# A log-sum-exp kernel: the wait for the final store moved behind the exit barriers, and the store halved over two queues

## The chip, the cores and the metric

The kernel runs on one core of a Trainium2 chip. The metric is device time in microseconds (us). All runs quoted here are of the fast state, at a granted clock of 1.0. The span in a profile is the time from the first to the last record of one profiled execution. It is about 1.8 us shorter than the time of the same execution (162.2 against 163.96 us for the kernel before), as it leaves out what happens before and after the records.

The engines are named as in the profile: ACT is ScalarE, DVE is VectorE, POOL is GpSimd, SP is SyncE. A name with a q (ACTq, SPq, POOLq) is the instruction queue of that engine, which issues transfers and handles semaphores. A semaphore is a counter that an engine or a transfer raises and that another engine waits on. A packet is one record of a DMA engine at work on a piece of a transfer. A store has landed when the last of its 16 increments has arrived at its semaphore. A drain is the DRAIN instruction that the exit puts ahead of each of an engine's reports.

Times are compared with the kernel before of the same rounds. Each run left one profiled execution, so a duration read from records is that of one execution.

## The reference

```python
# x: 32 x 512 x 1024 float32, axis = -1
x_max = np.max(x, axis=axis, keepdims=True)
return x_max.squeeze(axis) + np.log(np.sum(np.exp(x - x_max), axis=axis))
```

The output is 32 x 512 float32, that is 64 KB. The input is 64 MB. The kernel leaves the maximum out and takes the log of the sum of the exponentials directly.

## The kernel before

Rows are spread as 128 partitions x 128 rows. SyncE loads chunks of rows into a ring. ScalarE takes the exponentials and part of the sums, VectorE the other sums. ScalarE takes the log of the first 67 columns in mid-run and of the last 61 columns at the end, and stores all 128 columns with one transfer. GpSimd waits for it.

```python
    landed = [tc.alloc_semaphore(f"landed{i}") for i in range(len(CHUNKS))]
    act_done = tc.alloc_semaphore("act_done")
    dve_done = tc.alloc_semaphore("dve_done")
    stored = tc.alloc_semaphore("stored")
    # ... (loads, exponentials and sums: the change does not touch them)
    take_logs(logged, NB, dves, acts)          # the last Ln
    nc.scalar.wait_ge(act_done, acts)
    nc.scalar.dma_start(out=out_v, in_=res).then_inc(stored, 16)
    nc.gpsimd.wait_ge(stored, 16)
```

What the text does not show is the exit that the framework appends when its context closes. In the built kernel it reads, for every engine but GpSimd: drain, report to GpSimd, wait for release, and then the same again. GpSimd gathers the reports, releases the others, sets the semaphores that came from `tc.alloc_semaphore` to zero with one range clear, and then gathers and releases a second time. As GpSimd's wait for the store stands ahead of all that GpSimd does there, its part of the exit starts when the store has landed (161.215 us in the trace; the wait is passed at 161.239).

The softmax here doesn't subtract the row's maximum and nothing guards it: scores larger than these inputs give would overflow.

Of the kernel before, what the change touches and what calls it, by code (L numbers as in the profile page):

```python
# [1 line left out]

# [4 lines left out]



CHUNKS = [  # L10
    (4, 1), (15, 11), (16, 10), (16, 15), (16, 0), (14, 0), (12, 9), (9, 5), (7, 5), (5, 4),
    (4, 3), (3, 0), (2, 2), (2, 2), (1, 0), (1, 0), (1, 0),
]
RING_ROWS = 51

LN_AT = 5

FIRST_PARTS = [("sync", 0, 128)]


@with_exitstack
def kernel(
    ctx: ExitStack,
    tc: tile.TileContext,
    x: bass.AP,
    axis: bass.AP,
    out: bass.AP,
):
    nc = tc.nc
    P = nc.NUM_PARTITIONS  # L30

    assert axis in (-1, len(x.shape) - 1), f"only last-axis reduction supported, got {axis}"

    x_flat = x.flatten_outer_dims()
    N, D = x_flat.shape
    assert N % P == 0
    NB = N // P
    assert sum(r for r, _ in CHUNKS) == NB

    fp32 = mybir.dt.float32  # L40
    Exp = mybir.ActivationFunctionType.Exp
    Ln = mybir.ActivationFunctionType.Ln
    AX = mybir.AxisListType.X

    x_v = x_flat.rearrange("(p t) d -> p t d", p=P)
    out_v = bass.AP(tensor=out.tensor, offset=out.offset, ap=[[NB, P], [1, NB]])

    ring = nc.alloc_sbuf_tensor("ring", [P, RING_ROWS, D], fp32).ap()
    sums = nc.alloc_sbuf_tensor("sums", [P, NB], fp32).ap()
    res = nc.alloc_sbuf_tensor("res", [P, NB], fp32).ap()  # L50

    landed = [tc.alloc_semaphore(f"landed{i}") for i in range(len(CHUNKS))]
    act_done = tc.alloc_semaphore("act_done")
    dve_done = tc.alloc_semaphore("dve_done")
    stored = tc.alloc_semaphore("stored")


    hook = nc.pop_inst_callback()
    symbolic, nc._always_lower_symbolic_ap = nc._always_lower_symbolic_ap, False


    place = []
    row = slot = 0
    for r, _ in CHUNKS:
        if slot + r > RING_ROWS:
            slot = 0
        place.append((slot, row))
        slot += r
        row += r



    busy = [(0, 0)] * RING_ROWS
    acts = dves = 0

    def load(i):
        (s, row), r = place[i], CHUNKS[i][0]
        act_wait = max(a for a, _ in busy[s : s + r])
        dve_wait = max(d for _, d in busy[s : s + r])
        if dve_wait:  # L80
            nc.sync.wait_ge(dve_done, dve_wait)
        if act_wait:
            nc.sync.wait_ge(act_done, act_wait)
        for engine, lo, hi in FIRST_PARTS if i == 0 else [("sync", 0, P)]:
            getattr(nc, engine).dma_start(
                out=ring[lo:hi, s : s + r], in_=x_v[lo:hi, row : row + r]
            ).then_inc(landed[i], 16)

    def take_logs(lo, hi, dve_wait, act_wait):
        nonlocal acts  # L90
        nc.scalar.wait_ge(act_done, act_wait)
        nc.scalar.wait_ge(dve_done, dve_wait)
        nc.scalar.activation(out=res[:, lo:hi], in_=sums[:, lo:hi], func=Ln).then_inc(  # L93
            act_done, 1
        )
        acts += 1

    body = nc.main_func.blocks[-1]
    assert not body.instructions
    load(0)  # L100
    n_early = len(body.instructions)

    nc.scalar.preload_act_table_set("natural_log_exp_and_others")  # L103

    logged = 0
    done_before = [(0, 0)]
    for i, (r, n_dve) in enumerate(CHUNKS):
        if i:
            load(i)
        s, row = place[i]  # L110
        if i == LN_AT:
            logged = row
            take_logs(0, logged, *done_before[i])
        nc.scalar.wait_ge(landed[i], 16 * (len(FIRST_PARTS) if i == 0 else 1))
        if n_dve:
            nc.scalar.activation(  # L116
                out=ring[:, s : s + n_dve], in_=ring[:, s : s + n_dve], func=Exp
            ).then_inc(act_done, 1)
            acts += 1
            nc.vector.wait_ge(act_done, acts)  # L120
            nc.vector.reduce_sum(  # L121
                out=sums[:, row : row + n_dve], in_=ring[:, s : s + n_dve], axis=AX
            ).then_inc(dve_done, 1)
            dves += 1
            for j in range(n_dve):
                busy[s + j] = (0, dves)
        for j in range(n_dve, r):
            nc.scalar.activation(  # L128
                out=ring[:, s + j],
                in_=ring[:, s + j],  # L130
                func=Exp,
                accum_out=sums[:, row + j : row + j + 1],
            ).then_inc(act_done, 1)
            acts += 1
            busy[s + j] = (acts, 0)
        done_before.append((dves, acts))

    take_logs(logged, NB, dves, acts)
    nc.scalar.wait_ge(act_done, acts)
    nc.scalar.dma_start(out=out_v, in_=res).then_inc(stored, 16)  # L140
    nc.gpsimd.wait_ge(stored, 16)



    first = nc.main_func.blocks[0]
    head, work = first.instructions, body.instructions
    end = next(k for k, i in enumerate(head) if i.opcode == "UnconditionalBranch")
    head, tail = head[:end], head[end:]
    for ins in work[:n_early]:
        at = next(  # L150
            k for k, i in enumerate(head) if i.engine == ins.engine and i.opcode == "Drain"
        )
        head.insert(at, ins)
    first.instructions = head + work[n_early:] + tail
    body.instructions = []

    nc._always_lower_symbolic_ap = symbolic
    nc.push_inst_callback(hook)


# [1 line left out]
_INS = ['x', 'axis']  # L162
_OUTS = [((32, 512), 'float32')]

_NUMBERS = {'axis': -1}


# [26 lines left out]
```

## Time and profile before

Before the prediction: 164.2 us, the median of three runs (164.1 to 164.22).

| what | number | where it is read |
|---|---|---|
| bytes, mean rate | 67.18 MB at 414 GB/s | DMA part of the page |
| chain that ended last | ScalarE 52%, loads 38%, VectorE 7% | chain part of the page |
| end of the last Ln | 159.61 us | timeline |
| issue of the store to its last landing | 1.57 us | records of the store |
| last landing to the end of the span | 0.96 us | records of the exit |

The first line below is from the head of the page of the kernel before, the next from its chain part.

```profile
span 162.2 us, 213 instructions
...
ACT 52%; DMA 38%; DVE 7%; issue 1%
```

In this chain, loads take most of the time up to 83.7 us, and from there to the last Ln it is ScalarE. The change works behind it. The end of the timeline of the kernel before (start us, duration us, engine, line, operation):

```profile
159.14 0.19 ACT L128 ACTIVATION_READ_ACCUMULATOR ring<-ring 128x1 f32 x1
159.36 0.25 ACT L93 ACTIVATE res<-sums 128x61 f32<-128x61 f32 x1
159.64 0.37 ACTq L140 DMA_DIRECT2D out_dram<-res  x1
```

The timeline stops at the store's issue, 2.5 us before the end of the span. The rest is seen in the view of one source line, here L189, which has all instructions of the exit (duration ns min/median/max, first and last start us):

```profile
L189 POOLq EVENT_SEMAPHORE  x4: 17/17/17, 161.5 to 162.1; - x4
...
L189 POOLq DRAIN  x3: 34/41/83, 161.4 to 161.9; - x3
...
L189 ACTq DRAIN  x2: 8/80/152, 160.1 to 161.7; - x2
...
L189 POOLq COMPARE_BRANCH  x1: 33/33/33, 161.2 to 161.2; - x1
L189 POOLq EVENT_SEMAPHORE_RANGE_CLEAR  x1: 139/139/139, 161.7 to 161.7; - x1
```

POOLq passes its wait for the store with the branch at 161.2 us. All its drains, its four barrier steps and the range clear come after that. The view of the store alone, for the kernel before:

```profile
L140 ACTq DMA_DIRECT2D out_dram<-res x1: 369/369/369, 159.6 to 159.6; - x1
...
DMA to landing us min/median/max: 1.6/1.6/1.6
```

The single records of the same trace give the tail in nanosecond steps (us from the start of the span):

```
159.612          the last Ln ends
159.643-160.012  ScalarE issues the store
160.052-160.204  ScalarE drains (ahead of the first barrier)
160.515-160.869  the store's packets: 128 of 512 bytes, 16 of 4 bytes
161.038-161.215  the 16 semaphore increments of the store arrive
161.239          GpSimd passes the wait for the store
161.551          first release
161.744-161.883  range clear on GpSimd
162.074          second release
162.179          end of the last record
```

So 0.964 us (162.179 less 161.215) of exit work stand in line behind the landing.

### The profile page before, as it was taken

The numbers are of one execution on the slowest core, as the hardware profiler recorded it, in microseconds if no ns is written. First come the engines' busy times: TensorE is split into PE (matmuls) and PEld (weight loads), VectorE is DVE, ScalarE is ACT, GpSimd is POOL, SyncE is SP. The second block draws the span as 40 slices with busy tenths as digits, with TensorE's granted clock in tenths as the row PEclk, the third lists the DMA queues.
The fourth block names the chain that finished last, engine by engine and source line by source line (L and its number), as shares of the span: only waits on it lengthen the run. The fifth ranks groups of instructions, "written<-read, shape, count | busy, mean of one in ns | idle before, by whom it ended". The sixth has DMA issues, their size and how long they took to land.

```text
span 162.2 us, 213 instructions
## 1 busy us (share of the span) xinstructions
DVE 72.9 (45%) x11; ACT 124.1 (76%) x136; POOL 0.2 (0%) x4
## 2 busy tenths in 40 slices
DVE  0030000039960799000999900000006999799591
ACT  3180006997099971999339999999999999999993
POOL 0000000000000000000000000000000000000000
DMA  6999899969969959969988999999999999999970
GB/s 263 497 485 470 349 394 517 485 291 517 485 291 517 517 259 517 517 275 501 517 368 370 424 424 432 461 497 388 436 427 399 431 400 439 420 424 414 415 318 16
DMA packets 2593, 67.18 MB, mean 414 GB/s; under 512 B 288, under 2 KB 416, under 8 KB 800
## 3 DMA queue, kind: packets, MB, share of 16 engines
q1 hardware_dynamic: 2448, 67.11, 96.4%
q10 hardware_dynamic: 144, 0.07, 0.1%
q14 instruction: 1, 0.01, 0.0%
HBM read 67.11 MB, written 0.07 MB: 414 GB/s over the span
## 4 chain that ended last, share of the span: by engine, by line
ACT 52%; DMA 38%; DVE 7%; issue 1%
DMA ring<-in_x_dram 38%; ACT ring L128 30%; ACT ring L116 22%; DVE sums L121 7%; ACT res L93 0%
## 5 line engine op out<-in xcount | busy, mean ns | idle before, releaser
L121 DVE TENSOR_REDUCE sums<-ring 128x5 f32<-128x5120 f32 (+8 forms) x11 | 72.9, 6648 | 86.0 <-ACT ring L116 85.9
L116 ACT ACTIVATE ring<-ring 128x5120 f32<-128x5120 f32 (+8 forms) x11 | 59.3, 5394 | 29.4 <-DMA ring<-in_x_dram 29.4
L128 ACT ACTIVATE ring<-ring 128x1024 f32<-128x1024 f32 x61 | 63.4, 1041 | 5.3 <-DMA ring<-in_x_dram 5.3
L128 ACT ACTIVATION_READ_ACCUMULATOR ring<-ring 128x1 f32 x61 | 11.4, 187 | 0.0
L103 ACT ACT_TABLE_LOAD x1 | 1.3, 1283 | 0.8 <-PEq L175 0.8
L93 ACT ACTIVATE res<-sums 128x67 f32<-128x67 f32 (+1 forms) x2 | 0.5, 256 | 0.1
L175 POOL MEMSET const-bfloat16-1.0<- 128x1 bf16 x1 | 0.1, 101 | 0.0
L175 POOL MEMSET const-uint8-127<- 128x1 uint8 x1 | 0.1, 101 | 0.0
L175 POOL MEMSET const-float32-0.0<- 128x1 f32 x1 | 0.1, 98 | 0.2 <-issue 0.2
L175 POOL MEMSET const-float32-1.0<- 128x1 f32 x1 | 0.1, 98 | 0.0
## 6 DMA issues: line engine op xcount, KB each, us to landing
ring<-in_x_dram SPq DMA_DIRECT2D x1, 7680.0 KB, 24.8
ring<-in_x_dram SPq DMA_DIRECT2D x1, 7168.0 KB, 36.1
ring<-in_x_dram SPq DMA_DIRECT2D x1, 6144.0 KB, 21.6
ring<-in_x_dram SPq DMA_DIRECT2D x1, 4608.0 KB, 32.1
ring<-in_x_dram SPq DMA_DIRECT2D x2, 2048.0 KB, 26.3
ring<-in_x_dram SPq DMA_DIRECT2D x1, 3584.0 KB, 40.2
ring<-in_x_dram SPq DMA_DIRECT2D x1, 2560.0 KB, 44.4
ring<-in_x_dram SPq DMA_DIRECT2D x2, 1024.0 KB, 46.0
```

The lines of the kernel that those rows point to most:

```text
L93: nc.scalar.activation(out=res[:, lo:hi], in_=sums[:, lo:hi], func=Ln).then_inc(act_done, 1)
L103: nc.scalar.preload_act_table_set("natural_log_exp_and_others")
L116: nc.scalar.activation(out=ring[:, s : s + n_dve], in_=ring[:, s : s + n_dve], func=Exp).then_inc(act_done, 1)
L121: nc.vector.reduce_sum(out=sums[:, row : row + n_dve], in_=ring[:, s : s + n_dve], axis=AX).then_inc(dve_done, 1)
L128: nc.scalar.activation(out=ring[:, s + j], in_=ring[:, s + j], func=Exp, accum_out=sums[:, row + j : row + j + 1],).then_inc(act_done, 1)
L175: nc = _bacc.Bacc("TRN2", target_bir_lowering=False, num_devices=1)
```

## The change

The intent has two parts. The exit should run while the store is under way, so the wait for the store goes behind the second barrier; for this the semaphores are no longer the framework's, ScalarE sets them to zero after its issue, and GpSimd takes the store's semaphore back at the very end. And the store is cut into two halves of 64 partitions, issued at the same time by ScalarE and SyncE.

```diff
-    landed = [tc.alloc_semaphore(f"landed{i}") for i in range(len(CHUNKS))]
-    act_done = tc.alloc_semaphore("act_done")
-    dve_done = tc.alloc_semaphore("dve_done")
-    stored = tc.alloc_semaphore("stored")
+    landed = [nc.alloc_semaphore(f"landed{i}") for i in range(len(CHUNKS))]
+    act_done = nc.alloc_semaphore("act_done")
+    dve_done = nc.alloc_semaphore("dve_done")
+    sp_past = nc.alloc_semaphore("sp_past")
+    stored = nc.alloc_semaphore("stored")
+    used = sorted(sem.num for sem in [*landed, act_done, dve_done, sp_past])
  # ... (the load of the first chunk is written more simply, with the same effect)
     nc.scalar.wait_ge(act_done, acts)
-    nc.scalar.dma_start(out=out_v, in_=res).then_inc(stored, 16)
-    nc.gpsimd.wait_ge(stored, 16)
+    nc.sync.wait_ge(act_done, acts)
+    nc.sync.dma_start(out=out_v[P // 2 :], in_=res[P // 2 :]).then_inc(stored, 16)
+    nc.sync.sem_inc(sp_past, 1)
+    nc.scalar.dma_start(out=out_v[: P // 2], in_=res[: P // 2]).then_inc(stored, 16)
+    nc.scalar.wait_ge(sp_past, 1)
+    nc.scalar.sem_clear(range(used[0], used[-1] + 1))
  # ... 
+    tc.close()
+    tc.compile()
+    nc.gpsimd.wait_ge(stored, 32)
+    nc.gpsimd.sem_inc(stored, -32)
```

One thing is visible only in the built instructions. Some DMA issues carry a mark there ("precooked"). All 17 loads and the store of the kernel before carry it (this store took 369 ns to issue). The two half stores of 64 partitions do not. "Marked" and "unmarked" below mean this flag.

More of the change, by code (lines that the diff above doesn't have):

```diff
@@ L16 @@
 LN_AT = 5
-FIRST_PARTS = [("sync", 0, 128)]
 @with_exitstack
@@ L50 @@
     res = nc.alloc_sbuf_tensor("res", [P, NB], fp32).ap()
-    landed = [tc.alloc_semaphore(f"landed{i}") for i in range(len(CHUNKS))]
-    act_done = tc.alloc_semaphore("act_done")
-    dve_done = tc.alloc_semaphore("dve_done")
-    stored = tc.alloc_semaphore("stored")
+    landed = [nc.alloc_semaphore(f"landed{i}") for i in range(len(CHUNKS))]
[4 more added lines that the diff above has]
+    used = sorted(sem.num for sem in [*landed, act_done, dve_done, sp_past])
+    assert used == list(range(used[0], used[0] + len(used)))
     hook = nc.pop_inst_callback()
@@ L83, in load @@
             nc.sync.wait_ge(act_done, act_wait)
-        for engine, lo, hi in FIRST_PARTS if i == 0 else [("sync", 0, P)]:
-            getattr(nc, engine).dma_start(
-                out=ring[lo:hi, s : s + r], in_=x_v[lo:hi, row : row + r]
-            ).then_inc(landed[i], 16)
+        nc.sync.dma_start(out=ring[:, s : s + r], in_=x_v[:, row : row + r]).then_inc(
+            landed[i], 16
+        )
     def take_logs(lo, hi, dve_wait, act_wait):
@@ L113 @@
             take_logs(0, logged, *done_before[i])
-        nc.scalar.wait_ge(landed[i], 16 * (len(FIRST_PARTS) if i == 0 else 1))
+        nc.scalar.wait_ge(landed[i], 16)
         if n_dve:
```

## The prediction

> **What bounds the kernel now.** It streams 67.11 MB at 414 GB/s (DMA part of the page); the chain that ended last is 52% ScalarE, 38% loads, 7% VectorE. As built, each engine's order is the same up to the last Ln, so only the tail can move. Read from the raw records of the last 3 us (span ends at 162.18):
>
> - 159.36, last Ln, 253 ns; 159.64, ScalarE issues the store, 369 ns.
> - Store packets run 160.52 to 160.87 (144 of them); semaphore increments arrive 161.04 to 161.215. Issue to landing is 1.57 us.
> - GpSimd's wait for the store ends at 161.24, then the exit follows serially: first barrier released 161.55, other engines go on at 161.60, GpSimd drain 83 ns, semaphore range clear 139 ns, drain 34 ns, second barrier released 162.07, last record ends 162.18.
>
> So 0.96 us of the span, from landing to end, is exit work serial behind the store.
>
> **What the change does.**
> 1. Removes the wait for the store ahead of the barriers. Both barriers then run while the store flies. From ScalarE's issue: its drain (done 0.2 us after the issue ends), first release 0.1 us later, second 0.3 us after that (0.52 now, less GpSimd's clear and drain).
> 2. Moves the range clear (139 ns on GpSimd) to ScalarE, behind the issue and SyncE's flag. This delays ScalarE's arrival by about 0.2 us, but under the store's 1.57 us.
> 3. Adds, after the second barrier, a wait for 32 and one semaphore decrement on GpSimd: from landing to end about 0.12 us (24 ns to pass the wait, an 80 ns step as between GpSimd's barrier instructions, 17 ns).
> 4. Halves the store over two queues. The packets take only 0.35 of the 1.57 us, so at best about 0.1 us. [...] Against it, the compiler marks all 18 transfers of before with one issue form (precooked) and leaves the two half stores unmarked. I expect a longer issue: 0.5 to 0.7 us where the trace has 0.37 (a guess; the trace has no such case). Net: the store lands about 0.1 us later, near 161.3.
>
> **On the critical path.** Barriers would end near 161.0 to 161.15, the store lands near 161.3, end near 161.4: the store still ends last, 0.96 us behind it becomes about 0.12, and about 0.1 is given back by the issue. Gain about 0.75 us of 164.2, which is 0.5%. Predicted 163.4 us, range 163.0 to 163.8. Faster by over 2%: 0.01; within 2%: 0.98; slower by over 2%: 0.01.
>
> **What would show it.** (1) In the list of waits and the raw records: GpSimd's wait for the store begins after the second release and ends last; landing to end 0.1 to 0.15 us. (2) Range clear on ScalarE, about 0.14 us, ending before 160.7. (3) Two stores issued within 0.1 us of each other, each issue over 0.45 us (if 0.37, the gain is nearer 0.9). (4) All instruction durations before 159.6, and the GB/s row, unchanged within 0.3 us.
>
> **What would make it wrong.** The barrier chain could outlast the store if ScalarE arrives late (slow issue, slow clear), then halving the store buys nothing and the gain falls towards 0.5. What lies outside the profiled span (163.96 against 162.18 us) may overlap with the early exit of the other engines, for a larger gain. Drift of 0.1 to 0.2 us in the load phase is as large as the small terms.

0.96 us less 0.12 and 0.1 is 0.74, given as about 0.75 us. The 0.5 to 0.7 us for an unmarked issue were a guess; measured later were 0.525 and 0.557.

## The result, and the profile after

Ratios in this document are from the fast runs of both kernels in the same rounds. They are not quite the ratios of the medians quoted beside them.

The changed kernel took 163.94 us (median of six runs, 163.59 to 164.32). The kernel before took 164.21 us (six runs, 163.94 to 164.43). The ratio is 0.9986, with a 95% interval of 0.997 to 1.0002. The output is correct. The predicted class "within 2%" holds, but the predicted time of 163.4 us and its range of 163.0 to 163.8 do not: about a third of the predicted gain of 0.75 us arrived (0.0014 x 164.2 = 0.23 us, and at the most 0.5 by the interval). The interval includes 1, so by these times alone a gain is not shown; later rounds with more runs, below, show one.

The same views for the changed kernel. First its page, then the end of its timeline:

```profile
span 161.7 us, 214 instructions
...
ACT 52%; DMA 38%; DVE 7%; issue 1%
```

```profile
159.30 0.25 ACT L93 ACTIVATE res<-sums 128x61 f32<-128x61 f32 x1
159.58 0.53 SPq L141 DMA_DIRECT2D out_dram<-res  x1
159.59 0.56 ACTq L143 DMA_DIRECT2D out_dram<-res  x1
```

The body is unchanged: the last Ln starts at 159.30 us where it had started at 159.36. The two issues begin together, but each takes over 0.5 us where the single one had taken 0.37. The views of the store, of the range clear (L147), of the exit (L167) and of the final wait (L169) of the changed kernel:

```profile
L141 SPq DMA_DIRECT2D out_dram<-res x1: 525/525/525, 159.6 to 159.6; - x1
L143 ACTq DMA_DIRECT2D out_dram<-res x1: 557/557/557, 159.6 to 159.6; - x1
...
DMA to landing us min/median/max: 1.8/1.9/2.1
```

```profile
L147 ACTq EVENT_SEMAPHORE_RANGE_CLEAR  x1: 115/115/115, 160.2 to 160.2; - x1
```

```profile
L167 POOLq EVENT_SEMAPHORE  x4: 17/17/17, 160.8 to 161.2; - x4
...
L167 ACTq DRAIN  x2: 8/230/452, 160.3 to 161.0; - x2
```

```profile
L169 POOLq EVENT_SEMAPHORE  x1: 17/17/17, 161.7 to 161.7; - x1
```

The four barrier steps of POOLq that stood at 161.5 to 162.1 us now stand at 160.8 to 161.2, ahead of the landing. Only one instruction of 17 ns, at 161.7 us, comes after it. That part of the change did what was intended. But the slower half of the store needs 2.1 us from issue to landing where the whole store had needed 1.6. The single records:

```
159.554          the last Ln ends
159.580-160.105  SyncE issues its half       159.585-160.142  ScalarE issues its half
160.187-160.302  range clear on ScalarE
160.345-160.797  ScalarE drains
160.746-161.049  SyncE's packets (80)        161.030-161.323  ScalarE's packets (80)
161.235          second release
161.341          last record of the second barrier ends
161.665          the last of the 32 increments arrives
161.706          end of the last record
```

The sum over the tail, from the issue to the end: before, 1.572 + 0.964 = 2.536 us; changed, 2.085 + 0.041 = 2.126 us. The exit behind the landing gave back 0.92 us, the store took 0.51 us of it. The remaining gain is 0.41 us in the traces, and the 0.23 us of the times agrees with it within their interval.

### The profile page after: what moved, and what is told of

The parts are those of the page before. It is cut to its first block, busy times and chain, and to the rows that moved or that the text cites. A ratio compares the mean times of both kernels' runs of the same rounds, so it can differ in the third digit from the quotient of the medians.

```text
span 161.7 us, 214 instructions
## 1 busy us (share of the span) xinstructions
DVE 72.9 (45%) x11; ACT 124.0 (77%) x136; POOL 0.2 (0%) x4
## 4 chain that ended last, share of the span: by engine, by line
ACT 52%; DMA 38%; DVE 7%; issue 1%
DMA ring<-in_x_dram 38%; ACT ring L128 30%; ACT ring L116 22%; DVE sums L121 7%; ACT res L93 0%
```

## The experiments

The theory, formed from the records above, has two parts. First, an unmarked issue costs about 0.3 us more up to the first packet than a marked one (1.166 us for SyncE's half in the changed kernel, 0.872 for the store of before). Second, with two unmarked issues at the same time, the second queue's packets wait about 0.3 us for those of the first (1.450 us for ScalarE's half, against 1.166). The rivals were: the unmarked form alone explains everything (ScalarE's is just slow); the sharing by two queues alone explains everything; or the early barriers and the range clear on ScalarE slow the store, and not the halving.

All edits are against the changed kernel unless said otherwise. The first four ran on the same chip in the same rounds, where before took 164.15 us (median of 9). No run differs from the kernel before by more than 1%; what is compared here are ratios with their intervals, and the records of the tail.

### The changed exit with one marked store

```diff
-    nc.sync.wait_ge(act_done, acts)
-    nc.sync.dma_start(out=out_v[P // 2 :], in_=res[P // 2 :]).then_inc(stored, 16)
     nc.sync.sem_inc(sp_past, 1)
-    nc.scalar.dma_start(out=out_v[: P // 2], in_=res[: P // 2]).then_inc(stored, 16)
+    nc.scalar.dma_start(out=out_v, in_=res).then_inc(stored, 16)
  # and GpSimd waits for 16 and takes 16 back
```

> The changed exit with one store of 128 partitions on the ScalarE queue, as before had it (marked issue form); SyncE only raises its flag. Two-part theory (the unmarked form of the 64-row stores costs about 0.3 us up to the first packet[...]): issue 0.37 us, issue to last landing back to 1.57 us, landing to end 0.04 us, span about 161.2, time 0.9 us under before. Rival 1 (only the form) and rival 2 (only the sharing by two queues) expect the same here. Rival 3 (the early barriers, or the range clear on ScalarE, slow the store): landing stays near 2.1 us and the gain near 0.3.

It took 163.25 us, ratio to before 0.9941 (0.9929 to 0.9954), so about 0.97 us less. The views of its store and of its exit:

```profile
L141 ACTq DMA_DIRECT2D out_dram<-res x1: 371/371/371, 159.8 to 159.8; - x1
...
DMA to landing us min/median/max: 1.6/1.6/1.6
```

```profile
L164 ACTq DRAIN  x2: 8/8/8, 160.4 to 160.6; - x2
```

Issue to landing is 1.58 us again, landing to end 0.041. The barriers and the clear run beside the store and do not slow it, which rules out the third rival. The second release, at 160.80 us, is 0.56 us ahead of the landing at 161.36, so the barriers have room to spare. Without the split, the change of the exit gives about what steps 1 to 3 of the prediction had said.

### The same store, unmarked

```diff
+    nc.dge_precook = False
     nc.scalar.dma_start(out=out_v, in_=res).then_inc(stored, 16)
+    nc.dge_precook = True
```

This is against the kernel of the last experiment. Shape, queue and exit are the same, and only the flag differs (the built instructions of the two, compared, show no other difference than line numbers).

> As whole_act, same shape and queue, but the store alone built without the mark. Two-part theory: issue about 0.55 us, first packet about 1.17 us after the issue starts (0.87 with the mark), landing about 1.85 us, time 0.25 to 0.3 us over whole_act. Rival 1 (form alone explains the whole 0.5 us): landing about 2.1 us. Rival 2 (form costs nothing): landing 1.57 us and time as whole_act.

It took 163.62 us, ratio to before 0.9967 (0.9955 to 0.998), so 0.37 us more than the marked store by the medians. This is a little over what had been expected, as are the first packet and the landing below.

```profile
L142 ACTq DMA_DIRECT2D out_dram<-res x1: 555/555/555, 160.1 to 160.1; - x1
...
DMA to landing us min/median/max: 1.9/1.9/1.9
```

The issue takes 0.18 us longer (555 against 371 ns), but the first packet comes 0.34 us later (1.211 us after the start of the issue against 0.873), and so does the landing (1.919 against 1.579). The form costs 0.34 us, so the rival by which it costs nothing is wrong, and so is the one by which it costs the whole 0.5 us. The issue's own length shows little more than half of what the form costs.

### Only ScalarE's half

```diff
-    nc.sync.wait_ge(act_done, acts)
-    nc.sync.dma_start(out=out_v[P // 2 :], in_=res[P // 2 :]).then_inc(stored, 16)
  # and GpSimd waits for 16 and takes 16 back
```

Its output is wrong, which doesn't matter for the time.

> As the changed kernel, but only ScalarE's half of the store is issued (half of the output is wrong on purpose). Two-part theory: without the other queue's half, first packet about 1.17 us after the issue starts instead of 1.445, landing about 1.75 to 1.8 us instead of 2.08. Rival 1 (ScalarE's unmarked form is slow by itself): 1.44 and 2.08 us as with both halves. Rival 2: first packet near 0.87, landing near 1.5 us.

It took 163.55 us (ratio to before 0.9961, 0.9949 to 0.9974).

```profile
L141 ACTq DMA_DIRECT2D out_dram<-res x1: 555/555/555, 159.9 to 159.9; - x1
...
DMA to landing us min/median/max: 1.9/1.9/1.9
```

Alone, ScalarE's half sends its first packet 1.206 us after its issue and lands after 1.853 us; beside SyncE's half these are 1.445 and 2.08 us. So the other queue's half adds 0.23 us to the landing, and ScalarE's unmarked issue is not slow in itself. Both parts of the theory are needed: 1.57 to 1.85 by the form (already less the 0.07 us by which the half landed before the whole unmarked store, 1.853 against 1.919), 1.85 to 2.08 by the second queue.

### Only the split, with the exit of before

Against the kernel before:

```diff
-    nc.scalar.dma_start(out=out_v, in_=res).then_inc(stored, 16)
-    nc.gpsimd.wait_ge(stored, 16)
+    nc.sync.wait_ge(act_done, acts)
+    nc.sync.dma_start(out=out_v[P // 2 :], in_=res[P // 2 :]).then_inc(stored, 16)
+    nc.scalar.dma_start(out=out_v[: P // 2], in_=res[: P // 2]).then_inc(stored, 16)
+    nc.gpsimd.wait_ge(stored, 32)
```

> The exit of before, with only the store split by partitions over the two queues; GpSimd waits for 32 and then does the whole exit. All three theories: landing about 2.08 us after the issue, 0.96 us from landing to end, span about 162.6, time 0.4 to 0.5 us over before. If the split were harmless with the old exit (rival 3: the exit does the damage), time as before.

It took 164.62 us, ratio to before 1.0028 (1.0014 to 1.0041), that is 0.46 us longer. Issue to landing is 2.086 us and landing to end 0.964: the split's cost and the exit's length are each as they were, so the two parts of the change add up.

```profile
L141 SPq DMA_DIRECT2D out_dram<-res x1: 525/525/525, 159.8 to 159.8; - x1
L142 ACTq DMA_DIRECT2D out_dram<-res x1: 553/553/553, 159.8 to 159.8; - x1
...
DMA to landing us min/median/max: 1.8/2.0/2.1
```

```profile
L189 ACTq DRAIN  x2: 8/314/621, 160.4 to 162.3; - x2
```

ScalarE's drain behind the issue takes 621 ns here, and ends at 161.00 us, 0.23 us before ScalarE's first packet at 161.23.

### The changed kernel and the single store again

> The changed kernel unaltered, to have it in the same rounds as the other runs of this call. Issue to landing 2.08 us again, landing to end 0.04 us; from the trace 0.3 to 0.5 us under before.

> The changed exit with one marked store on ScalarE, unaltered, in the same rounds as the changed kernel: 1.57 us to landing, 0.5 us under the changed kernel and 0.9 under before. If it is not at least 0.3 us under the changed kernel, the split is not what ate the gain.

These two, the marked column halves and the first run of the single store on SyncE (both below) ran in the same rounds (before: 164.34 us). The changed kernel took 163.95 us, ratio 0.9978 (0.9966 to 0.9991), so here its gain of 0.36 us is clear of noise. The single store took 163.46 us, ratio 0.995 (0.9938 to 0.9963), 0.45 us under the changed kernel by the means. The landings were 2.094 and 1.567 us after the issue, which is a difference of 0.53. The split, as it was built, is what ate the gain.

### Halved by columns: two queues, both marked

Halves of 64 columns have 128 partitions, and both are marked in the built kernel.

```diff
-    nc.sync.dma_start(out=out_v[P // 2 :], in_=res[P // 2 :]).then_inc(stored, 16)
+    nc.sync.dma_start(out=out_v[:, NB // 2 :], in_=res[:, NB // 2 :]).then_inc(stored, 16)
     nc.sync.sem_inc(sp_past, 1)
-    nc.scalar.dma_start(out=out_v[: P // 2], in_=res[: P // 2]).then_inc(stored, 16)
+    nc.scalar.dma_start(out=out_v[:, : NB // 2], in_=res[:, : NB // 2]).then_inc(stored, 16)
```

> The changed kernel, but the store is halved by columns: two stores of 128 partitions and 256 bytes a row, both built with the mark. [...] one queue's packets begin 0.87 us after issue, the other's 0.3 us later or more, landing 1.85 to 2.0 us, time about 0.3 us over whole_act_again. Rival (only the unmarked form matters; the queues do not hinder each other): both begin at 0.87, landing 1.5 to 1.6 us, time as whole_act_again.

The numbers are an estimate for the case that the second of two marked stores also waits: 0.87 us is the first packet of a single marked store (0.872, 0.873), and 0.3 us the gap of the changed kernel (1.450 less 1.166).

```profile
L141 SPq DMA_DIRECT2D out_dram<-res x1: 349/349/349, 159.9 to 159.9; - x1
L143 ACTq DMA_DIRECT2D out_dram<-res x1: 382/382/382, 159.9 to 159.9; - x1
...
DMA to landing us min/median/max: 1.5/1.6/1.7
```

It took 163.43 us, ratio 0.9949 (0.9936 to 0.9963), the same as the single store within the noise. The landing came 1.662 us after the issue. That lies between the two expectations, and the first, which was mine, was the worse of them: the second queue's packets do begin later than the first's, but by 0.110 us (0.954 against 0.844) instead of 0.3, and then the two streams overlap: when ScalarE's first packet began, 15 of SyncE's were under way. So a second queue does not wait 0.28 us in every case. Either the gap is short with the marked form, or it is long with the halving by partitions. The next run tells these apart.

### Halved by columns, unmarked

```diff
+    nc.dge_precook = False
  # ... the two column halves as above
+    nc.dge_precook = True
```

> The two column halves of cols, but both built without the mark. If the wait of the second queue for the first belongs to the unmarked form: first packets at about 1.2 us on one queue and 1.45 to 1.5 on the other, 0.28 us apart as in the changed kernel (0.11 in cols), landing 2.1 us or a little more, time 0.4 us over cols. If it belongs to the halving by partitions instead: both queues 0.1 us apart near 1.2 us, landing about 1.95 us.

It took 164.10 us (before, in these rounds: 164.55), ratio 0.9975 (0.996 to 0.9991). By the ratios that is 0.0026 x 164.5 = 0.43 us over the marked column halves (which ran on another chip), where 0.4 had been expected. The views of its store and of its exit:

```profile
L142 SPq DMA_DIRECT2D out_dram<-res x1: 545/545/545, 160.3 to 160.3; - x1
L144 ACTq DMA_DIRECT2D out_dram<-res x1: 584/584/584, 160.3 to 160.3; - x1
...
DMA to landing us min/median/max: 1.8/1.9/2.1
```

```profile
L168 ACTq DRAIN  x2: 8/224/440, 161.1 to 161.7; - x2
```

First packets came at 1.189 and 1.462 us, 0.273 us apart, and the last landing at 2.075. These are the numbers of the changed kernel with twice the rows in each half. So the long wait of the second queue (0.27 us instead of 0.11) belongs to the unmarked form, not to the halving by partitions, and it did not grow with the number of rows in a half.

The tail of all runs, from the single records (us from the start of the first store issue; where there are two queues, SyncE's first packet stands first):

| store | marked | issue, ns | first packets | last landing | landing to end |
|---|---|---|---|---|---|
| before: one, ScalarE | yes | 369 | 0.872 | 1.572 | 0.964 |
| changed: 2 x 64 partitions | no | 525, 557 | 1.166, 1.450 | 2.085 | 0.041 |
| one, ScalarE | yes | 371 | 0.873 | 1.579 | 0.041 |
| one, ScalarE | no | 555 | 1.211 | 1.919 | 0.042 |
| one half of 64 partitions | no | 555 | 1.206 | 1.853 | 0.041 |
| 2 x 64 partitions, exit of before | no | 525, 553 | 1.174, 1.443 | 2.086 | 0.964 |
| 2 x 64 columns | yes | 349, 382 | 0.844, 0.954 | 1.662 | 0.041 |
| 2 x 64 columns | no | 545, 584 | 1.189, 1.462 | 2.075 | 0.042 |
| one, SyncE | yes | 348 | 0.844 | 1.551 | 0.042 |

### One marked store on SyncE, and the finished columns stored early

```diff
  # in both, the two half stores of the changed kernel are taken out (not shown)
  # whole_sp: the single store from SyncE; GpSimd waits for 16 and takes 16 back
     nc.sync.wait_ge(act_done, acts)
+    nc.sync.dma_start(out=out_v, in_=res).then_inc(stored, 16)
     nc.sync.sem_inc(sp_past, 1)
  # early_sp: the columns of the first Ln when they are done, the others at the end
  # (first_log is the count of act_done right after that first Ln)
+    nc.sync.wait_ge(act_done, first_log)
+    nc.sync.dma_start(out=out_v[:, :logged], in_=res[:, :logged]).then_inc(stored, 16)
     nc.sync.wait_ge(act_done, acts)
+    nc.sync.dma_start(out=out_v[:, logged:], in_=res[:, logged:]).then_inc(stored, 16)
     nc.sync.sem_inc(sp_past, 1)
```

> The changed exit with one marked store on the SyncE queue. SyncE's marked issue takes 0.33 us in the loads where ScalarE's takes 0.37: landing 1.53 to 1.57 us after the issue, time within 0.1 us of whole_act_again. If ScalarE's later drain and the clear mattered, it would be lower by more than 0.1.

> whole_sp unaltered, for the same rounds as the candidate: 0.9 us under before, landing 1.55 us after the issue.

> A candidate: both stores on SyncE and marked; the 67 finished columns are stored while the engines still work on the rest, and only 61 columns (244 bytes a row) after the last Ln. Packets of 244 bytes should take about 17 ns each where 512 bytes take 27 (cols has 16 to 18 for 256 bytes), 8 for each engine: issue to landing about 1.48 us against 1.55 in whole_sp, so about 0.07 us under whole_sp, too little for the times to show. If the early store disturbs the loads, the last Ln comes later and the time is above whole_sp.

The single store on SyncE took 163.44 us, ratio 0.9945 (0.9933 to 0.9958), and in the later rounds 163.56, ratio 0.994 (0.9927 to 0.9953). Its landing came after 1.551 and 1.544 us. It is the same as the single store on ScalarE within the noise.

The early store took 163.33 us, ratio 0.9929 (0.9916 to 0.9941), with its final part landing after 1.452 us. That is 0.09 us under the single SyncE store of the same rounds by the records. The times say 0.18 us, but their intervals overlap, so only the 0.09 us is shown. Its early issue lasted 23.4 us in SyncE's queue, as the view of its stores shows, and landed at 158.5 us, just behind the last load. It did no visible harm: all loads had been issued ahead of it, and the last Ln ended at 159.91 us against 160.03 in the single SyncE store of the same rounds.

```profile
L142 SPq DMA_DIRECT2D out_dram<-res x1: 23374/23374/23374, 113.0 to 113.0; - x1
L144 SPq DMA_DIRECT2D out_dram<-res x1: 343/343/343, 159.9 to 159.9; - x1
```

All four kernels with the changed exit and marked stores (one on ScalarE, one on SyncE, column halves, early columns) beat both the kernel before and the changed one. For the early columns this is read from the ratios to before (0.9929 against 0.9978 and 0.9986), as they did not run in the same rounds as the changed kernel.

## Why the prediction was wrong

The mechanism was right and one term was mis-sized.

- **The wait behind the barriers (steps 1 and 3).** Right. Predicted from landing to end: 0.12 us; measured 0.041. Wait and decrement had been merged into one instruction of 17 ns, so the step of 80 ns that was counted between them does not exist.
- **The range clear on ScalarE (step 2).** Right. Predicted about 0.14 us, ending before 160.7; measured 115 ns, ending at 160.30, and off the critical path (the last record of the barriers ends at 161.341, the store lands at 161.665).
- **The end of the barriers.** Predicted 161.0 to 161.15 us, measured 161.34. ScalarE's drain behind an unmarked issue took 452 ns instead of 152 (8 ns behind the range clear when the issue was marked). As the store was later still (161.665 us), this cost nothing.
- **The split (step 4).** This is the step that failed: "Net: the store lands about 0.1 us later, near 161.3." It landed 0.51 us later (2.085 us after the issue instead of 1.572). The length of the issue was guessed right (0.5 to 0.7 us; measured 0.525 and 0.557). Two things were missed. The cost of the form was taken as the added length of the issue (0.18 us for the same store), while the first packet moves by 0.34 us. And the two halves were taken to run side by side, while the second one's packets began 0.28 us after the first one's and its landing came 0.23 us later than alone. The prediction gave two issues at once no microseconds of their own.
- **The sum.** Predicted 0.96 - 0.12 - 0.1 = 0.74 us. With the measured terms it is 0.964 - 0.041 - 0.513 = 0.41 us. The predicted 163.4 us is about what the kernel without the split took (163.25 and 163.46).

The split alone cost 0.46 us (ratio 1.0028). The time that the packets need does not explain it. In an estimate from the trace of the changed kernel, 64 packets of 32 ns (the mean in SyncE's half), spread evenly over the 16 engines of the page, keep each engine busy for 4 x 32 = 128 ns, while the second half's packets began 0.28 us after the first's. The packet records bear this out: up to 16 packets were under way at once, but only one when ScalarE's first packet began, and 79 of SyncE's 80 had started by then. So the second half's packets began late while few others were under way. What held them back was not shown.

What stays open: why the first packet comes later after an unmarked issue, why the second of two unmarked stores begins so late, and why the 64 partitions were left unmarked, no run shows. No run has a marked store of 64 partitions: in every kernel built here, such a store is unmarked.

## What to carry to other kernels

Wait for the last store at the very end of the program, not ahead of an exit that needs no result: here that was worth the 0.9 us that the exit takes, and the barriers then ran under the store. Here the kernel then set the semaphores to zero itself, all but the store's with one range clear of 115 ns on ScalarE. Cut a final store only after looking at what the compiler makes of the pieces; here a store without the mark landed 0.34 us later (1.919 against 1.579), and the second of two unmarked stores issued together sent its first packet 0.27 to 0.28 us after the first one's. Judge a transfer by the first packet and the landing, not by the length of its issue (0.18 us longer here, for a landing 0.34 us later), and cost each half of a change by itself, since a gain of 0.9 and a loss of 0.5 look like a small gain.

## What else the records show

- Of the 1.572 us from issue to landing of the store of the kernel before, 0.872 passed before the first packet, 0.354 in packets, and 0.346 from the end of the last packet to the last increment.
- ScalarE's drain ahead of the exit's first barrier took longer when the store was unmarked. With the range clear between issue and drain, it took 8 ns (marked), 229 to 230 ns (one unmarked) and 440 to 452 ns (two unmarked). Directly behind the issue it took 152 ns (one marked) and 621 ns (two unmarked). In the changed kernel it held up the barrier: it ended at 160.797 us, the last of the engines' drains there, and GpSimd's first barrier step followed at 160.830.
- The semaphore range clear took 139 ns on GpSimd in the kernel before and 115 ns on ScalarE in the changed one.
